# Two convolution tiles moved from retention into the merge, and layer 1's retention low parts moved to VectorE

## The chip, the cores and the metric

The kernel runs on one core of a Trainium2 chip. The metric is the device time of one execution in microseconds (us). Before the change three runs took 2858.27, 2862.72 and 2868.04 us; the median is 2862.72. The engines that matter here are TensorE (PE in the rows: matmuls), VectorE (DVE), ScalarE (ACT) and GpSimd (POOL). Each works through its own list of instructions in a fixed order.

## The reference

The reference is a two-layer transformer for diffusion. The token stream has 256 latent and 256 context rows of 1024 channels. In each layer one projection of the modulated stream feeds three mixing branches: a retention with 8 heads in two directions, an attention, and a convolution. The branches are gated, projected and summed; then comes a mixture of 64 small experts. What the change touches are the first and the third branch:

```python
scores = jnp.einsum('bnihd,bnjhd->bnhij', qc, kc) * decay_in          # retention, per head
y_inner = jnp.einsum('bnhij,bnjhe->bnihe', scores, vc)
...
br_ret = (jax.nn.silu(g) * layernorm_per_head(y)) @ w_ret_o

def conformer_conv(u, w_dw, b_dw, ln_g, ln_b):
    a, gte = jnp.split(u, 2, axis=-1)
    glu = a * jax.nn.sigmoid(gte)
    y = depthwise_conv(glu, w_dw, width=31) + b_dw                    # 1024 channels
    return jax.nn.silu(layer_norm(y, ln_g, ln_b))                     # norm over all channels

out = (sigmoid(g_ret) * br_ret + sigmoid(g_att) * br_att + sigmoid(g_conv) * (conv @ w_conv_o)) @ w_out
```

Layer 0 computes all 512 rows, layer 1 in the branches only the 256 latent ones (context rows enter as keys and values).

## The kernel before

*Weights in two parts.* Every float32 weight comes from memory as a piece `raw` of 128 partitions. ScalarE copies its high part to `whi` (L90), and VectorE or GpSimd subtracts that to give the low part `wlo` (L91), 128x1024 at a time. A matmul in L228 is then three matmuls: high by high, high by low, low by high. Which engine makes the low parts is set by a count: inside `split_on_pool(n)` every n-th low part goes to GpSimd, with n = 1 all of them, with n = 0 none. `SHARE` holds n for retention ("ret") and attention ("att"), one number for each layer; the merges of retention and convolution run under `split_on_pool(3)`.

*Retention* (L607 on) goes through 8 heads in four pairs. For a pair it projects keys, queries, values and a gate; for each head VectorE makes two decay masks (`ml` L619, `m2` L620, added by GpSimd in L621 and L629, exponentials by ScalarE in L622), multiplies the scores by them (`sa`, L683), and scales and splits the head's output (`ry` L696 and L697, `bT` L91). TensorE's mean of squares of a head is L693. After each pair the function yields, and the caller places work of the convolution there.

*Convolution.* The 1024 channels are eight tiles of 128. `conv_tile(t)` projects a tile (48 matmuls), gates it (`G`, L565, two buffers) and has VectorE run 31 taps over it: L569 and then 30 times L572, summed in one PSUM buffer `cacc`, the last into `cy`. The taps carry a lower priority than the rest (`CONV_BACK`), so the scheduler fills VectorE's list with them where other work has none. When all eight are there, `conv_norm` sums the tiles on GpSimd (`csum`, L584 and L586), takes the mean on TensorE (L580), subtracts it (L589), squares (L591), adds (L593), takes the second mean (L580), and scales (L597) and activates (L598). `conv_out` splits the result into parts, and the merge of the convolution reads them.

*The merge.* `merge(0, ...)` projects retention's output in four steps, each with a gate and a part of the adaLN projection. The norm of the convolution is placed ahead of its last step (L471). Then `merge(2, ...)` does the same with the convolution's output.

*The order of the work.* The program's order gives priorities; a scheduler turns these into one fixed list per engine when the kernel is built. So moving a call moves instructions on every engine. In layer 1 the weights' buffers are those of the whole kernel, in layer 0 the merge adds some of its own.

Of the kernel before, what the change touches and what calls it, by code (L numbers as in the profile page):

```python
# [31 lines left out]

ADA = {(0, 0): 2, (0, 2): 2, (0, 1): 0, (1, 0): 1, (1, 1): 0, (1, 2): 0}

SHARE = {"ret": (1, 1), "att": (1, 2)}
LN_EXP = list(get_activation_tables("")).index("natural_log_exp_and_others")

CAPS = {0: [256] * 2 + [192] * 7 + [128] * 19 + [64] * 36, 1: [192] + [128] * 11 + [64] * 52}
# [31 lines left out]
def body(ctx, tc, A, out):  # L70
# [12 lines left out]
    def pool_of(name, side=None):  # L83
        return tc.tile_pool(name=name, bufs=1, reuse_waits="tile", side=side)
# [11 lines left out]
    @contextmanager  # L96
    def split_on_pool(every):

        share.append(share[0])
        share[0] = every  # L100
        yield
        share[0] = share.pop()

    @contextmanager
    def weight_pool(name, raw, parts, own=False):


        with tc.tile_pool(name=name, bufs=1, reuse_waits="tile") as p:
            WP.append(dict(pool=p, raw=raw, parts=parts, own=own))
            yield  # L110
            WP.pop()
# [31 lines left out]
    def slab(ap):  # L143
        return chunk(ap, 4)
# [61 lines left out]
    def open_aux(n):  # L206

        aux_scope.close()
        aux_scope.enter_context(aux_banks(n))
# [3 lines left out]
    def bank(tag="mm", bufs=1):  # L213
        if tag == "mm":
            mm_turn[mms[-1]] = i = mm_turn.get(mms[-1], -1) + 1
            tag = f"mm{mms[-1][i % len(mms[-1])]}"
        pool_, bufs = aux[-1] if tag == "aux" else (ps, bufs)
        return pool_.tile([128, 512], F32, name=tag, tag=tag, bufs=bufs)

    def mm(o, a, b, start, stop):  # L220

        ops = []
        for x, y in zip(a, b):
            ops += [(x[0], y[0]), (x[0], y[1])]
            if len(x) == 2:
                ops.append((x[1], y[0]))
        for i, (l_, r_) in enumerate(ops):
            pe.matmul(o, l_, r_, start=start and i == 0, stop=stop and i == len(ops) - 1)  # L228
# [80 lines left out]
    def some(n):  # L309

        if n and later:
            ada(*later[:n])
            del later[:n]
            if not later:
                last_modulation()
# [47 lines left out]
    def actt(name):  # L363
        return wk.tile([128, 512], F32, name=name, tag="act", bufs=3)
# [29 lines left out]
    def row(name):  # L394
        return wk.tile([128, D], F32, name=name, tag="row", bufs=4)
# [23 lines left out]
    def mix(l):  # L419
        hT = [(hb[:, k], hb[:, 8 + k]) for k in range(8)]  # L420
        NQ = 512 if l == 0 else T
        NT = NQ // 128
        NS = NQ // T

        def wi(s):
            return ready.pop((l, s), None) or slab(A["w_in"][l * 38 + s])

        def wo(i, s):
            return slab(A["w_o"][(l * 4 + i) * 4 + s])

        def projT(w, n):

            o = [bank(), bank()]
            for h in range(2):
                for c in range(2):
                    mm(o[c][:, :n], [tuple(z[:, k, c * 128:c * 128 + 128] for z in w[h]) for k in range(4)],
                       [tuple(z[:, :n] for z in hT[4 * h + k]) for k in range(4)], h == 0, h == 1)
            return o

        def proj(w, src, nt):  # L440

            o = [bank().rearrange("p (a b) -> p a b", a=2) for _ in range(nt // 2)]
            for t in range(nt):
                for h in range(2):
                    mm(o[t // 2][:, t % 2], [tuple(z[:, t * 128:t * 128 + 128] for z in src[4 * h + k]) for k in range(4)],
                       [tuple(z[:, k] for z in w[h]) for k in range(4)], h == 0, h == 1)
            return o

        merged, sigmoids = [], {}
        with pool_of(f"mix{l}") as M:  # L450
            def newT():
                return [tuple(M.tile([128, NQ], FR, name="bT", tag="bT", bufs=16) for _ in range(2)) for _ in range(8)]

            def gates(br, s):

                gate = projT(wi(S_GT + br * 4 + s), NQ)
                sg = []
                for i in range(2):
                    sg.append(actt("sg")[:, :NQ])
                    sigmoids[i] = act.activation(sg[i], gate[i][:, :NQ], AF.Sigmoid)  # L460
                return sg

            def keep_gate(s, gate):

                sg = actt("sg")[:, :NQ]
                act.activation(sg, gate[:, :NQ], AF.Copy)
                sp.dma_start(gd[s, :, :NQ], sg)

            def merge(br, bT, between=None):
                for s in range(4):  # L470
                    if between and s == 3:  # L471
                        between()
                    if br == 1:
                        sg = []
                        for i in range(2):
                            sg.append(actt("sg")[:, :NQ])
                            act.dma_start(sg[i], gd[2 * s + i, :, :NQ])
                            act.activation(sg[i], sg[i], AF.Sigmoid)
                    else:
                        sg = gates(br, s)  # L480
                        some(ADA[l, br])
                    w = wo(br, s)
                    b = [bank(), bank()]
                    for h in range(2):
                        for c in range(2):
                            mm(b[c][:, :NQ], [tuple(z[:, k, c * 128:c * 128 + 128] for z in w[h]) for k in range(4)],
                               [bT[4 * h + k] for k in range(4)], h == 0, h == 1)
                    for i in range(2):
                        if len(merged) < 8:
                            if i == 0:  # L490
                                mg = row("mg")
                            m = mg[:, i * NQ:i * NQ + NQ]
                            dve.tensor_tensor(m, b[i][:, :NQ], sg[i], op=OP.mult)
                            merged.append(m)
                        else:
                            m = merged[2 * s + i]
                            dve.tensor_tensor(sg[i], b[i][:, :NQ], sg[i], op=OP.mult)
                            (dve if br == 1 and s == 3 else pool).tensor_tensor(m, m, sg[i], op=OP.add)
                    some(ADA[l, br])

            open_aux(1)
            with pool_of(f"conv{l}") as PC:
                conv_tile, conv_norm, conv_out = conv(l, PC, NQ, NS, lambda t: projT(wi(S_CU + t), NQ), newT)
                with pool_of(f"ret{l}") as P, split_on_pool(SHARE["ret"][l]):
                    bT = newT()
                    for p in retention(l, P, NQ, NS, NT, lambda s, nt: proj(wi(s), hT, nt),
                                       lambda s: projT(wi(s), NQ), bT):
                        conv_tile(2 * p)
                        conv_tile(2 * p + 1)
                with weight_pool(f"w_merge{l}", *((2, 3), (0, 0))[l]), split_on_pool(3):  # L510
                    merge(0, bT, conv_norm)
                    merge(2, conv_out(newT()))
            open_aux(2)
            with pool_of(f"att{l}") as P, split_on_pool(SHARE["att"][l]):
                bT = newT()
                attention(l, P, NQ, NS, NT, bT, hT, keep_gate, sigmoids.values())
                merge(1, bT)

        return merged
# [1282 lines left out]
    for t in range(4):  # L1802
        for c in range(2):
            p = bank("tr", 2)
# [15 lines left out]
    for l in range(L):  # L1820
        with weight_pool(f"w_mix{l}", l, l):
            merged = mix(l)
        moe(l, merged, A["tokens"] if l == 0 else xd)
# [89 lines left out]
```

## Time and profile before

| | before |
|---|---|
| median of 3 runs | 2862.72 us (2858.27 to 2868.04) |
| profiled execution | 2861.13 us |
| its span, first to last instruction | 2859.3 us |
| mean granted clock of TensorE | 0.944 |
| TensorE busy | 2582.9 us, 90% |
| VectorE busy | 1660.0 us, 58% |
| ScalarE busy | 1307.7 us, 46% |
| GpSimd busy | 673.6 us, 24% |

The profiled execution has 1.8 us outside its span. "Busy" is the time in which an engine has an instruction running; an instruction that is held up while it runs counts as busy. The granted clock is the share of TensorE's full 2.4 GHz that the chip let it have; 0.5 is its lower level of 1.2 GHz. Retention of layer 0 lies at about 90 to 346 us, its first merge to 441; in layer 1 they lie at 1695 to 1905 and on to 1969.

### The profile page before, as it was taken

How to read it: one execution, taken by the hardware profiler on the slowest of the kernel's cores; microseconds unless marked ns; L12 is line 12 of the kernel's file. 1: busy time of each engine (PE TensorE's matmuls, PEld its weight loads, DVE VectorE, ACT ScalarE, POOL GpSimd, SP SyncE). 2: the span in 40 equal slices, each digit the busy share in tenths (PEclk: the TensorE clock that was granted, in tenths of full speed). 3: DMA queues.
4: the chain of work that ended last, by engine and by line, in shares of the span. 5: the costliest groups of instructions: out<-in, count | busy, mean ns of one | idle time of the engine just before them, and what ended most of it. 6: DMA issues, size and time to landing. Idle time of an engine off the chain costs nothing. (4 is left out here: it accounts for less than half of the span.)

```text
span 2859.3 us, 39759 instructions
## 1 busy us (share of the span) xinstructions
PE 2582.9 (90%) x14811; PEld 1872.1 (65%) x14811; DVE 1660.0 (58%) x2963; ACT 1307.7 (46%) x2388; POOL 673.6 (24%) x449
## 2 busy tenths in 40 slices
PE   6999999999997899999999478888989799999995
PEld 5887777788777655555555268877978655554552
DVE  4588895258847555555555487887587722231223
ACT  3444425247732355555555236445476333343331
POOL 2444311222234111212121045532312300000000
PEclk7999999999998899999999798889999899999997
DMA  5212256621162599999999742235415399999996
GB/s 217 74 60 74 97 204 229 235 77 52 63 207 82 219 373 401 405 391 393 397 379 391 297 168 89 89 118 193 163 65 183 121 389 420 419 366 397 416 415 255
DMA packets 130055, 685.18 MB, mean 240 GB/s; under 512 B 22080, under 2 KB 37056, under 8 KB 56896
## 3 DMA queue, kind: packets, MB, share of 16 engines
q1 hardware_dynamic: 103344, 624.80, 56.1%
q0 software_dynamic: 20496, 41.98, 3.9%
q10 hardware_dynamic: 6016, 15.80, 1.4%
q8 instruction: 119, 1.95, 0.3%
q14 instruction: 80, 0.66, 0.1%
HBM read 651.76 MB, written 62.98 MB: 250 GB/s over the span
## 5 line engine op out<-in xcount | busy, mean ns | idle before, releaser
L90 ACT ACTIVATE whi<-raw 128x1024 fp32r<-128x1024 f32 x444 | 457.6, 1053 | 266.3 <-PE mm L228 149.9
L91 POOL TENSOR_TENSOR wlo<-raw,whi 128x1024 fp32r<-128x1024 f32 x140 | 344.4, 2469 | 723.3 <-ACT whi L90 653.8
L91 DVE TENSOR_TENSOR wlo<-raw,whi 128x1024 fp32r<-128x1024 f32 x304 | 375.0, 1254 | 204.1 <-ACT whi L90 200.7
L228 PE MATMUL mm<-whi,hb 128*128 128x256 f32 (+1 forms) x2080 | 428.9, 302 | 34.1 <-ACT whi L90 9.2
L228 PE MATMUL mm<-hb,whi 128*128 128x512 f32 (+1 forms) x1536 | 402.2, 349 | 14.8 <-ACT whi L90 6.0
L228 PEld LDWEIGHTS mm<-whi,hb 128*128 128x128 f32 x2080 | 349.7, 202 | 45.0 <-issue 14.2
L1544 PE MATMUL mm<-raw,xw 128*64 128x512 f32 x1408 | 332.8, 600 | 0.9 <-DMA raw<-in_w_exp 0.9
L1614 POOL DMA_INDIRECT y<-y,ix x94 | 95.7, 1018 | 977.8 <-ACT y L1610 867.1
L228 PE MATMUL mm<-wlo,hb 128*128 128x256 f32 (+1 forms) x1040 | 312.9, 301 | 11.4 <-POOL wlo L91 7.9
L228 PEld LDWEIGHTS mm<-hb,whi 128*128 128x128 f32 x1536 | 269.6, 195 | 51.8 <-ACT whi L90 6.6
L572 DVE SCALAR_TENSOR_TENSOR cacc<-G,cpk,cacc 128x512 f32<-128x512 f32 (+1 forms) x464 | 287.4, 619 | 10.3
L228 PE MATMUL mm<-hb,wlo 128*128 128x512 f32 (+1 forms) x768 | 268.7, 351 | 4.2 <-POOL wlo L91 3.5
L228 PE MATMUL mm<-whi,xp 128*128 128x512 f32 x736 | 264.4, 413 | 1.7 <-ACT whi L90 1.7
L228 PEld LDWEIGHTS mm<-wlo,hb 128*128 128x128 f32 x1040 | 209.6, 202 | 15.8 <-POOL wlo L91 8.8
L1544 PEld LDWEIGHTS mm<-raw,xw 128*64 128x64 f32 x1408 | 94.4, 136 | 165.1 <-issue 158.2
L228 PE MATMUL mm<-bT,whi 128*128 128x512 f32 (+1 forms) x768 | 193.5, 342 | 0.6 <-DVE bT L91 0.2
L1106 DVE SCALAR_TENSOR_TENSOR hidp<-mm,tab,sgl 128x256 f32<-128x256 f32 x86 | 41.6, 483 | 237.0 <-ACT sgl L1102 236.1
L228 PEld LDWEIGHTS mm<-whi,xp 128*128 128x128 f32 x736 | 140.8, 191 | 51.0 <-ACT whi L90 9.4
L91 DVE TENSOR_TENSOR xp<-tr,xp 128x512 fp32r<-128x512 f32 (+2 forms) x126 | 59.6, 492 | 192.7 <-ACT xp L90 161.3
L1610 ACT ACTIVATE y<-mm 128x512 f32<-128x512 f32 (+1 forms) x188 | 110.3, 594 | 130.6 <-PE mm L1601 69.5
L228 PE MATMUL mm<-wlo,xp 128*128 128x512 f32 x400 | 161.6, 404 | 7.1 <-DVE wlo L91 6.9
L228 PEld LDWEIGHTS mm<-hb,wlo 128*128 128x128 f32 x768 | 149.5, 195 | 24.7 <-POOL wlo L91 4.4
(654 smaller groups left out, 4357.0 us busy)
## 6 DMA issues: line engine op xcount, KB each, us to landing
raw<-in_w_exp SPq DMA_DIRECT2D x384, 1024.0 KB
raw<-in_w_in SPq DMA_DIRECT2D x76, 1024.0 KB
raw<-in_w_ada SPq DMA_DIRECT2D x48, 1024.0 KB
raw<-in_w_o SPq DMA_DIRECT2D x32, 1024.0 KB
yb<-y SPq DMA_DIRECT2D x24, 1024.0 KB
mod<-modrow SPq DMA_DIRECT2D x12, 512.0 KB
raw<-in_w_shared SPq DMA_DIRECT2D x6, 1024.0 KB
x1d<-xr ACTq DMA_DIRECT2D x6, 512.0 KB
```

Source lines behind the costliest of these rows:

```text
L90: act.activation(hi, src, AF.Copy)
L91: eng.tensor_tensor(lo, src, hi, op=OP.subtract)
L228: pe.matmul(o, l_, r_, start=start and i == 0, stop=stop and i == len(ops) - 1)
L572: dve.scalar_tensor_tensor(v(y if j == 30 else acc), G[:, :, j:j + T], cpk[:, t, j:j + 1], v(acc), op0=OP.mult, op1=OP.add)
L1106: dve.scalar_tensor_tensor(o[:n], b[:n, 256:512], gate[:n], sg[:n], op0=OP.mult, op1=OP.mult)
L1544: pe.matmul(os_[s][0][half], xhs[s][0](k)[:, half], raws[index[r, i // 2]][:, k % 4 * 512:k % 4 * 512 + 512], start=k == 0, stop=k == 7)
L1610: act.activation(ys[b][:n, c * 512:c * 512 + 512], o[c], AF.Copy)
L1614: pool.indirect_dma_start(out=y8s[s, b][:], in_=ys[b][:n], in_offset=None, out_offset=bass.IndirectOffsetOnAxis(ap=tabs[s][b][1][:n, 1:2], ...
```

## The change

One number in `SHARE` changes: in layer 1's retention no low part goes to GpSimd, all are made by VectorE. And the convolution's tiles are spread in another way, in both layers: before, two after each of the four pairs of heads; now two, one, two and one, and the last two tiles ahead of the first two steps of the retention's merge, where the low parts are shared by `split_on_pool(3)`. `conv_norm` stays ahead of the last step. From L515 on lines are 8 higher in the changed kernel (L580 becomes L588).

```diff
-SHARE = {"ret": (1, 1), "att": (1, 2)}
+SHARE = {"ret": (1, 0), "att": (1, 2)}
...
             def merge(br, bT, between=None):
                 for s in range(4):
-                    if between and s == 3:
-                        between()
+                    if between:
+                        between(s)
...
                     for p in retention(l, P, NQ, NS, NT, lambda s, nt: proj(wi(s), hT, nt),
                                        lambda s: projT(wi(s), NQ), bT):
-                        conv_tile(2 * p)
-                        conv_tile(2 * p + 1)
+                        for t in ((0, 1), (2,), (3, 4), (5,))[p]:
+                            conv_tile(t)
+
+                def rest(s):
+
+                    if s < 2:
+                        conv_tile(6 + s)
+                    if s == 3:
+                        conv_norm()
+
                 with weight_pool(f"w_merge{l}", *((2, 3), (0, 0))[l]), split_on_pool(3):
-                    merge(0, bT, conv_norm)
+                    merge(0, bT, rest)
                     merge(2, conv_out(newT()))
```

On VectorE, in the first pair of heads of layer 1's retention, this stands before the change (`vs`, `vc`, `vl` belong to the values, `ml`, `m2`, `sa`, `sal` to the masks and scores; the number behind a name tells its instance):

```order
L656 TENSOR_REDUCE vs_15840<-mm0_15735 128x4
L657 SCALAR_TENSOR_TENSOR vc_15841<-vs_15840,mm0_15735 128x512
L620 TENSOR_SCALAR m2_15913<-delta_15501,lgx_159 128x512
L91 TENSOR_TENSOR vl_15833<-vc_15841,vh_15832 128x512
L625 TENSOR_TENSOR ml_15911<-ml_15911,cst_78 128x128 x2
L683 SCALAR_TENSOR_TENSOR sa_15932<-tr_15925,ml_15503 128x512
L683 SCALAR_TENSOR_TENSOR sa_15951<-tr_15944,mx_15504 128x512
L619 TENSOR_SCALAR ml_15975<-delta_15501,lg_125 128x512
```

The same place with the change:

```order
L664 TENSOR_REDUCE vs_15840<-mm0_15735 128x4
L91 TENSOR_TENSOR wlo_16042<-raw_16039,whi_16041 128x1024
L665 SCALAR_TENSOR_TENSOR vc_15841<-vs_15840,mm0_15735 128x512
L628 TENSOR_SCALAR m2_15913<-delta_15501,lgx_159 128x512
L91 TENSOR_TENSOR wlo_16046<-raw_16039,whi_16045 128x1024
L91 TENSOR_TENSOR wlo_16141<-raw_16138,whi_16140 128x1024
L91 TENSOR_TENSOR vl_15833<-vc_15841,vh_15832 128x512
L691 SCALAR_TENSOR_TENSOR sa_15932<-tr_15925,ml_15503 128x512
L633 TENSOR_TENSOR ml_15911<-ml_15911,cst_78 128x128 x2
L691 SCALAR_TENSOR_TENSOR sa_15951<-tr_15944,mx_15504 128x512
L627 TENSOR_SCALAR ml_15975<-delta_15501,lg_125 128x512
```

Three low parts of weights, each behind a high part that ScalarE has to make first, now stand between the values and the first scores.

On VectorE, where layer 1's convolution ends (the last taps into `cy`, then the subtraction of the mean), before:

```order
L493 TENSOR_TENSOR mg_18459<-mm1_18409,sg_18373 128x256
L572 SCALAR_TENSOR_TENSOR cacc_17949<-G_17944,cpk_15480,cacc_17949 128x256 x2
L493 TENSOR_TENSOR mg_18459<-mm2_18410,sg_18375 128x256
L572 SCALAR_TENSOR_TENSOR cacc_17949<-G_17944,cpk_15480,cacc_17949 128x256
L276 TENSOR_TENSOR modT_117<-aux_18475,bT_ada_80 128x4
L572 SCALAR_TENSOR_TENSOR cacc_17949<-G_17944,cpk_15480,cacc_17949 128x256
L91 TENSOR_TENSOR wlo_18544<-raw_18541,whi_18543 128x1024
L572 SCALAR_TENSOR_TENSOR cacc_17949<-G_17944,cpk_15480,cacc_17949 128x256 x2
L572 SCALAR_TENSOR_TENSOR cy_17948<-G_17944,cpk_15480,cacc_17949 128x256
L589 TENSOR_TENSOR cy_16105<-cy_16105,aux_18488 128x256
```

And with the change:

```order
L580 SCALAR_TENSOR_TENSOR cacc_17854<-G_17849,cpk_15480,cacc_17854 128x256 x8
L580 SCALAR_TENSOR_TENSOR cy_17853<-G_17849,cpk_15480,cacc_17854 128x256
L91 TENSOR_TENSOR wlo_18625<-raw_18622,whi_18624 128x1024
L577 TENSOR_SCALAR cacc_18120<-G_18115,cpk_15480 128x256
L91 TENSOR_TENSOR wlo_18629<-raw_18622,whi_18628 128x1024
L580 SCALAR_TENSOR_TENSOR cacc_18120<-G_18115,cpk_15480,cacc_18120 128x256 x10
L91 TENSOR_TENSOR wlo_18750<-raw_18743,whi_18749 128x1024
L580 SCALAR_TENSOR_TENSOR cacc_18120<-G_18115,cpk_15480,cacc_18120 128x256 x19
L580 SCALAR_TENSOR_TENSOR cy_18119<-G_18115,cpk_15480,cacc_18120 128x256
L597 TENSOR_TENSOR cy_16105<-cy_16105,aux_18488 128x256
```

Before, the gated products `mg` of the merge's third step stand among the last tile's taps; now all 30 of the last tile stand behind them, and the low parts for the last gate and for the next branch stand among these taps.

On TensorE, at the mean over the squares (`crs`) of layer 1's convolution, before (`mm3`, `mm0` with `bT` are products of the merge's last step):

```order
L228 MATMUL mm3_18632<-bT_15499,whi_18628 128x256
L228 MATMUL mm3_18632<-bT_15500,whi_18628 128x256
L228 MATMUL mm3_18632<-bT_15499,wlo_18629 128x256
L580 MATMUL aux_18521<-crs_18480,mean_d_102 128x256
L228 MATMUL mm0_18633<-bT_15485,whi_18624 128x256
L228 MATMUL mm0_18633<-bT_15486,whi_18624 128x256
L228 MATMUL mm0_18633<-bT_15485,wlo_18625 128x256
```

And with the change (`mm2` with `hb` is a gate of the next branch):

```order
L228 MATMUL mm2_18753<-hb_15175,whi_18749 128x256 x2
L228 MATMUL mm2_18753<-hb_15175,wlo_18750 128x256
L588 MATMUL aux_18488<-csum_18479,mean_d_102 128x256
L588 MATMUL aux_18521<-crs_18480,mean_d_102 128x256
L228 MATMUL mm0_18633<-bT_15485,whi_18624 128x256
L228 MATMUL mm0_18633<-bT_15486,whi_18624 128x256
L228 MATMUL mm0_18633<-bT_15485,wlo_18625 128x256
```

Before, 45 rows of products stood between the mean over the channels (`csum`) and that over the squares; now these products, and the next gate, stand ahead of the first of the two means, and the second follows it directly.

## Rows read from the trace of the kernel before

**Rows 1.** Busy time of each engine in the whole span, with its share and instructions.
```profile
PE 2582.9 (90%) x14811; PEld 1872.1 (65%) x14811; DVE 1660.0 (58%) x2963; ACT 1307.7 (46%) x2388; POOL 673.6 (24%) x449
```
**Rows 2.** Windows: length, PE, PEld, DVE, ACT, POOL busy, granted clock, DMA share, GB/s.
```profile
90.00:346.00 256.00, 243.65 (x1315) 201.60 (x1315) 208.43 (x299) 113.03 (x148) 102.48 (x60) 0.95 0.20 70
...
1695.00:1905.00 210.00, 181.25 (x1282) 171.65 (x1282) 168.23 (x310) 114.89 (x160) 108.75 (x64) 0.88 0.26 90
1905.00:1969.00 64.00, 53.02 (x448) 47.27 (x448) 55.70 (x109) 18.70 (x29) 12.75 (x9) 0.89 0.52 188
1969.00:1996.00 27.00, 22.48 (x167) 19.75 (x168) 18.49 (x36) 25.31 (x42) 3.84 (x2) 0.94 0.45 164
```
**Rows 3.** VectorE groups, 1690 to 1905: busy, mean ns, idle before, releasers.
```profile
L91 DVE TENSOR_TENSOR bT<-ry,bT 128x256 fp32r<-128x256 f32 x7 | 9.7, 1386 | 0.4
...
L683 DVE SCALAR_TENSOR_TENSOR sa<-tr,ml 128x512 f32<-128x512 f32 x8 | 5.5, 683 | 6.7 <-POOL ml L621 6.7
```
**Rows 4.** GpSimd groups, 1690 to 1905.
```profile
L91 POOL TENSOR_TENSOR wlo<-raw,whi 128x1024 fp32r<-128x1024 f32 x35 | 86.2, 2479 | 83.2 <-ACT whi L90 66.1 <-issue 15.2 <-POOL mx L629 1.0
L621 POOL TENSOR_TENSOR ml<-ml,m 128x512 f32<-128x512 f32 x8 | 11.4, 1424 | 0.4 <-POOL wlo L91 0.4
```
**Rows 5.** Timeline, GpSimd and VectorE: start us, us, engine, line, operation, idle before.
```profile
1695.80 2.40 POOL L91 TENSOR_TENSOR wlo<-raw,whi 128x1024 fp32r<-128x1024 f32 x1 [0.81 <-DVE rtmp L412]
1698.62 1.35 POOL L621 TENSOR_TENSOR ml<-ml,m 128x512 f32<-128x512 f32 x1 [0.42 <-POOL wlo L91]
...
1695.86 2.63 DVE L620 TENSOR_SCALAR m<-delta,lgx 128x512 f32<-128x512 f32 x1
1698.41 0.41 DVE L413 TENSOR_TENSOR z<-z,rtmp 128x256 f32<-128x256 f32 x1
...
1719.16 0.49 DVE L620 TENSOR_SCALAR m<-delta,lgx 128x512 f32<-128x512 f32 x1
```
**Rows 6.** Waits of TensorE, 1695 to 1905: total us, times, longest.
```profile
PE tr L228 <- DVE sa L683: 8.2, 5, 4.6
```
**Rows 7.** Timeline of VectorE around layer 1's first merge.
```profile
1905.30 0.42 DVE L696 TENSOR_TENSOR ry<-mm,rs 128x256 f32<-128x256 f32 x1
...
1910.16 1.22 DVE L91 TENSOR_TENSOR wlo<-raw,whi 128x1024 fp32r<-128x1024 f32 x1
1911.30 5.21 DVE L572 SCALAR_TENSOR_TENSOR cacc<-G,cpk,cacc 128x256 f32<-128x256 f32 x10
...
1967.45 0.48 DVE L572 SCALAR_TENSOR_TENSOR cy<-G,cpk,cacc 128x256 f32<-128x256 f32 x1
1969.60 0.75 DVE L589 TENSOR_TENSOR cy<-cy,aux 128x256 f32<-128x256 f32 x2 [1.67 <-PE aux L580]
```
**Rows 8.** Timeline of TensorE at layer 1's two means and behind.
```profile
1968.86 0.70 PE L580 MATMUL aux<-csum,mean_d 128*128 128x256 f32 x2 [0.29 <-POOL csum L586]
...
1977.40 0.70 PE L580 MATMUL aux<-crs,mean_d 128*128 128x256 f32 x2
...
1995.71 0.39 PE L228 MATMUL mm<-bT,whi 128*128 128x256 f32 x2
```
**Rows 9.** Timeline of VectorE, layer 0: last head's scaling, last tap.
```profile
346.13 0.69 DVE L696 TENSOR_TENSOR ry<-mm,rs 128x512 f32<-128x512 f32 x1 [0.33 <-ACT rs L243]
...
435.20 0.74 DVE L572 SCALAR_TENSOR_TENSOR cy<-G,cpk,cacc 128x512 f32<-128x512 f32 x1
```
**Rows 10.** Timeline of TensorE, layer 0's merge: matmuls, and the mean.
```profile
392.46 0.63 PE L228 MATMUL mm<-hb,whi 128*128 128x512 f32 x2
...
393.16 0.63 PE L228 MATMUL mm<-hb,whi 128*128 128x512 f32 x2
...
440.39 1.02 PE L580 MATMUL aux<-csum,mean_d 128*128 128x512 f32 x2
```
**Rows 11.** Waits of VectorE, 1900 to 2070.
```profile
DVE wlo L91 <- ACT whi L90: 24.6, 15, 4.6
```
**Rows 12.** VectorE groups, 1905 to 1970.
```profile
L91 DVE TENSOR_TENSOR wlo<-raw,whi 128x1024 fp32r<-128x1024 f32 x8 | 12.9, 1621 | 0.7 <-ACT whi L90 0.7
```

## The prediction, made before the changed kernel ran

> **What bounds the kernel now.** I read the page's busy times first, then the mixing stages in a table by windows, then what stretches and what waits there, and last the timeline at the two places where the convolution ends.
>
> TensorE is busy 2582.9 us of the span, VectorE 1660.0 [rows 1]. The sum over the program therefore says TensorE, but the change touches four stretches only: retention of layer 0 (90 to 346 us) and of layer 1 (1695 to 1905), and the first merge behind each. The reader should see in [rows 2] how different the two layers are. Retention of layer 0 leaves TensorE 256.0 - 243.65 = 12.35 us idle. Retention of layer 1 leaves 210.0 - 181.25 = 28.75 us idle and runs at a granted clock of 0.88: both its own 256 columns and its waits are short, and VectorE's 168.2 us are nearly as long as TensorE's work. In the first merge of layer 1 VectorE is busy 55.7 of 64 us and is the one that is waited for: TensorE's mean over the channel sums stands at 1968.86 [rows 8], right behind the last tap, and all that follows of the convolution hangs on it.
>
> In retention of layer 1 some of VectorE's busy time is not work. GpSimd makes 35 low parts there in 86.2 us [rows 4]. While it made the one at 1695.80, VectorE's scaling of `delta` took 2.63 us; the same instruction took 0.49 at 1719.16 [rows 5]. The group `bT<-ry,bT` has a mean of 1.386 us, while the convolution's taps, of the same width and with their sum in PSUM, keep to ten in 5.21 [rows 7]. Summed over the order of VectorE's instructions at quiet prices (tap 0.52, low part 1.14, both from one start to the next [rows 7], the others at their quiet rows), retention up to the last head is 148.6 us of work; the busy time is 168.2 and the stretch 210: 19.6 us are stretched instructions and 41.8 us idle. Of the idle time 6.7 us end with GpSimd's sum of the decay mask, `sa<-POOL ml` [rows 3]; that sum stood behind a low part in GpSimd's queue at 1695.80 and 1698.62 [rows 5]. TensorE in turn waits 8.2 us for `sa` [rows 6].
>
> The Trainium skill, "SBUF — State Buffer", section "SBUF: two separate sides", says that a GpSimd instruction and a VectorE instruction with two inputs in SBUF (or in a two-port mode) take one port pair as a lock, and the later one blocks for the whole of the other. Stretched subtractions beside unstretched taps agree with it. By that rule the 16 sums that GpSimd keeps could still block as much as they last.
>
> **The change, part by part.** First, low parts of layer 1's retention. In the new order 34 of them stand between VectorE's retention instructions; at 1.14 us that is 39 us more work on VectorE and 84 us less on GpSimd. GpSimd keeps two sums per head: eight took 11.4 us [rows 4], so I put all 16 at 22. What of the 19.6 us of stretch stays lies between 0 and those 22; I take 3, because the sum at 1698.62 stands beside an instruction of 0.41 us [rows 5].
>
> Second, the tiles. A tile is 48 matmuls and 31 taps. With 512 columns three matmuls start in 393.16 - 392.46 = 0.70 us [rows 10], so one is 0.233 us, and I take half, 0.117 us, for the 256 columns of layer 1. Counted in the two orders, 50 matmuls leave the stretch up to the last head of layer 0 (11.7 us), and 33 that of layer 1 (3.9 us). Fewer than two tiles' 96, since part of the last tile stood behind the last head already and other work moves up. VectorE's work behind the last head grows from 84.6 us (to the last tap) to 111.4 in layer 0, and from 54.9 to 84.0 in layer 1; before the last head of layer 1 it is 160.1 instead of 148.6: 39 us of low parts come and 27 us of taps and GLUs go.
>
> *Layer 0.* The last head's scaling is at 346.13, the last tap ends at 435.94 [rows 9]: 84.6 us of work took 89.8. With 111.4 I take 117.4. The head comes earlier by 11.7 us and by what TensorE no longer waits, 0 to 12.35; with 26 us less on VectorE before it I take 8 of these, in all 20. So the last tap ends at 346.1 - 20 + 117.4 = 443.5, and the mean follows after 0.9 as in layer 1 [rows 7, 8], at 444.4; before it was at 440.39 [rows 10], with the sum of channels lying ready. That is +4.0. Nine more matmuls stand in front of it, so 2.1 us less behind: +1.9. Bounds: +10 with nothing of the waits back, -2 with all.
>
> *Layer 1.* From the last head's scaling at 1905.30 to the first subtraction of the mean at 1969.60 [rows 7] are 64.3 us for 54.9 of work, 9.4 over. With 84.0 it is 93.4: +29.1. Against that stands how much earlier the last head comes. VectorE: 160.1 of work, 3 of stretch, and of 41.8 idle I leave 32 (6.7 go with GpSimd's queue, 3 come by the new waits below, and low parts fill some holes): 195 instead of 210, so 15 us. TensorE agrees with that size: 3.9 us of matmuls and 11 of its 28.75 idle. Bounds: 0, when new waits eat all, and 32, when 17 of the idle and half of what the clock takes (0.12 x 181 = 22 us) come back.
>
> Behind the mean the order on TensorE is new. Before, 45 rows stood between the mean over the channels and the mean over the squares, and they filled the 8.5 us between 1968.86 and 1977.40 [rows 8]. Now nothing stands between them: what did has moved ahead, so TensorE stands idle through both the wait for the last taps and this chain. In front of the mean are 80 more matmuls (9.4 us); of the 22.5 us of work between 1969 and 1996 [rows 2] 13.1 stay. From the mean to the first matmul of the convolution's output, 1995.71 - 1968.86 = 26.9 us, it becomes 8.5 + 13.1 = 21.6, where I take -4.5 as some waits stay, and +1 for TensorE's clock, which the windows show under its full level of 2.4 GHz where it waits (granted 0.88 in retention, 0.89 in the merge [rows 2]). Layer 1: 29.1 - 15 - 4.5 + 1 = +10.6.
>
> *New waits.* A low part on VectorE waits for ScalarE's high part, and with it all that is queued behind: taps, scores' `sa`, the head's scaling. Where VectorE is busy this cost 0.7 us for 8 pieces [rows 12], 0.09 each; where it is not, 24.6 us for 15 [rows 11], 1.64 each. For 34 that is 3 to 56 us. I take 3, the row in which VectorE is as full as it will be here.
>
> The Trainium skill, "Perfetto Trace Analysis", section "Optimizing Scalar/DVE Operations", advises to take work off a VectorE that is saturated, and adds that giving it to GpSimd may not help since both share a port. The change goes against the first half; the stretched rows speak for the second.
>
> **Sum.** The profiled execution took 2861.1 us, 1.6 under the median of the runs shown. 2861.1 + 1.9 + 10.6 = 2873.6; I forecast 2873.
>
> **Rivals.** *Relief* (other side). GpSimd's low parts cost more than their stretch: they hold back the decay sums, hence `sa`, hence TensorE and its clock. Place: retention of layer 1; price 17 us of idle, 11 of clock and the 3.9 moved, 32; layer 0 gets its waits back too. 29.1 - 32 - 4.5 = -7.4 and -2.1: 2851.6, say 2852. It decides from about 26 us on, where layer 1 comes out even. For it: waits for `sa` and the stretch are the largest items [rows 3, 6]. Against: VectorE would have to do 160 us of work in 178, with less idle than it has anywhere now.
>
> *Low parts at the head of VectorE's queue.* Each waits for its high part 0.35 us or more, between the two rows above; 12 us of that use up all that the stretch gave, and the last head stays at 1905. 29.1 - 4.5 + 1 + 1.9 = +27.5: 2889. For it: 24.6 us of such waits [rows 11]. Against: 0.7 us where VectorE was full [rows 12].
>
> *Nothing.* TensorE's work is the same, and what is moved fills holes elsewhere: 2861. Against it: VectorE's work up to the mean grows by 245.0 - 204.4 = 40.6 us in a stretch in which it is already waited for.
>
> **How the numbers follow.** Under 0.3% (8.6 us) a measurement of this kernel can't be told from no change, so faster is below 2854, slower above 2870. Forecast 0.45, own range 2862 to 2886: most of it slower (0.28), some the same (0.15), 0.02 faster. Relief 0.28: 0.25 faster, 0.03 the same. Head of queue 0.17: slower. Nothing 0.10: 0.08 the same, 0.02 faster. Together faster 0.29, same 0.26, slower 0.45. The range reaches from a little below relief to the head of queue, 2848 to 2891.
>
> **What would show it.** The window from layer 1's first decay to its last head 15 us shorter, VectorE's groups there back at quiet means (`bT<-ry,bT` near the 0.42 of the scaling beside it [rows 7]) and 34 low parts of 1.2 us; the time from the last head to the mean near 93 us instead of 64; TensorE idle some 8 us between its two means and about as long ahead of the first; in layer 0 the mean near 444. Wrong: waits of `wlo` for `whi` of more than 10 us in retention (head of queue), or a last head more than 26 us earlier (relief).

## The result: 0.63% slower, and the profile after

The changed kernel took 2880.82 us (median of 5 runs, 2879.68 to 2883.06) against 2864.81 for the kernel before beside it: a ratio of 1.0063, 95% interval 1.0048 to 1.0079, or 16 us. The forecast was 2873, slower, with 2848 to 2891 as the range. The profiled execution took 2882.63 us, 21.5 more than that of before. Where do these 21.5 us arise? I compare starts of the same instruction in the two timelines:

| | before | after | later by |
|---|---|---|---|
| layer 0, last head's scaling `ry` | 346.13 | 331.77 | -14.4 |
| layer 0, mean subtracted | 441.45 | 453.91 | +12.5 |
| layer 0, first sum of the experts' outputs, `yb` | 1606.41 | 1620.80 | +14.4 |
| layer 1, first decay | 1695.46 | 1707.72 | +12.3 |
| layer 1, last head's scaling | 1905.30 | 1888.28 | -17.0 |
| layer 1, mean subtracted | 1969.60 | 1986.87 | +17.3 |
| layer 1, last `aqT` of attention | 2147.17 | 2171.66 | +24.5 |
| layer 1, last sum of the experts' outputs, `yb` | 2842.61 | 2864.07 | +21.5 |

So in this pair of executions layer 0 loses about 14 us, and layer 1, from its first decay on, another 12 up to the last `aqT` and 9 up to the end. The last stretch, from there to the end, is the same code in every run here and takes 692 to 699 us, so these last 3 us are chance. In both layers the last head comes much earlier, and more than that is lost behind it.

The windows of the profile after, with bounds moved to the same events [rows 2] (length; PE, PEld, DVE, ACT, POOL busy; granted clock, DMA share, GB/s):

```profile
90.00:332.00 242.00, 233.07 (x1269) 194.31 (x1268) 187.33 (x271) 109.46 (x145) 92.68 (x54) 0.94 0.21 74
332.00:454.00 122.00, 111.55 (x619) 83.89 (x619) 109.36 (x149) 27.39 (x37) 21.79 (x14) 0.96 0.48 179
1708.00:1888.00 180.00, 166.01 (x1222) 156.85 (x1221) 155.94 (x293) 109.16 (x155) 31.11 (x25) 0.93 0.29 100
1888.00:1986.00 98.00, 75.02 (x584) 66.68 (x583) 81.57 (x161) 25.32 (x37) 20.68 (x17) 0.87 0.48 172
1986.00:2015.00 29.00, 14.29 (x87) 11.56 (x87) 12.28 (x34) 24.18 (x40) 0.52 (x1) 0.68 0.11 37
```

The reader is to see two things. Layer 1's retention (third row) became short and full: 180 us instead of 210, TensorE idle 14 instead of 28.75, granted clock 0.93 instead of 0.88. The two rows below pay for it: TensorE is idle 23 of 98 us and 15 of the next 29, where before it was idle 11 of 64 and 4.5 of the next 27.

VectorE's groups in layer 1's retention, with the low parts on it, from 1702 to 1888 (busy, mean ns, idle before, releasers):

```profile
L91 DVE TENSOR_TENSOR wlo<-raw,whi 128x1024 fp32r<-128x1024 f32 x33 | 43.7, 1326 | 7.0 <-ACT whi L90 7.0
...
L691 DVE SCALAR_TENSOR_TENSOR sa<-tr,ml 128x512 f32<-128x512 f32 x8 | 5.5, 683 | 2.6 <-POOL ml L629 2.6
...
L91 DVE TENSOR_TENSOR bT<-ry,bT 128x256 fp32r<-128x256 f32 x7 | 3.0, 432 | 0.5 <-ACT bT L90 0.3
```

`bT<-ry,bT` fell from 1386 to 432 ns and the wait for the mask from 6.7 to 2.6 us [rows 3]: most of the stretch is gone. The 33 low parts waited 7.0 us for their high parts.

Layer 0, TensorE at the first weights of the merge, and at the mean [rows 10]:

```profile
335.38 0.97 PE L228 MATMUL mm<-hb,whi 128*128 128x512 f32 x3 [2.25 <-ACT whi L90]
343.75 0.80 PE L228 MATMUL mm<-hb,wlo 128*128 128x512 f32 x1 [7.41 <-DVE wlo L91]
...
452.75 1.12 PE L588 MATMUL aux<-csum,mean_d 128*128 128x512 f32 x2 [0.29 <-POOL csum L594]
```

And VectorE over the same first stretch:

```profile
331.77 0.69 DVE L704 TENSOR_TENSOR ry<-mm,rs 128x512 f32<-128x512 f32 x1 [1.32 <-ACT rs L243]
...
336.28 6.29 DVE L580 SCALAR_TENSOR_TENSOR cacc<-G,cpk,cacc 128x512 f32<-128x512 f32 x8
342.48 1.22 DVE L91 TENSOR_TENSOR wlo<-raw,whi 128x1024 fp32r<-128x1024 f32 x1
...
453.91 1.29 DVE L597 TENSOR_TENSOR cy<-cy,aux 128x512 f32<-128x512 f32 x2 [2.64 <-PE aux L588]
```

At the mean itself TensorE waits only 0.29 us. It lost its time earlier: a low part of a moved tile's weights, made by VectorE now, stands in the list behind eight taps, and TensorE stood 7.41 us for it. Before, TensorE had no idle time at all from 346 to 441:

```profile
346.00:441.00 95.00, 95.00 (x561) 72.10 (x559) 83.85 (x116) 23.38 (x33) 17.90 (x10) 1.00 0.59 216
```

Layer 1, TensorE at the two means and at the first matmul of the convolution's output [rows 8]:

```profile
1985.61 1.22 PE L588 MATMUL aux<-csum,mean_d 128*128 128x256 f32 x2 [7.25 <-POOL csum L594]
1992.63 1.22 PE L588 MATMUL aux<-crs,mean_d 128*128 128x256 f32 x2 [5.80 <-DVE crs L601]
...
2013.20 1.01 PE L228 MATMUL mm<-bT,whi 128*128 128x256 f32 x3 [8.00 <-ACT whi L90]
```

Here TensorE does wait for the last taps (7.25), then for the squares (5.80), and then 8.00 for a high part of a weight that ScalarE made only behind the activations of the convolution:

```profile
2008.66 0.59 ACT L606 ACTIVATE cy<-cy,cpk 128x256 f32<-128x256 f32 x1
...
2010.22 1.28 ACT L460 ACT_TABLE_LOAD   x1
2011.52 0.39 ACT L460 ACTIVATE sg<-mm 128x256 f32<-128x256 f32 x1
2011.80 0.41 ACT L90 ACTIVATE bT<-cy 128x256 fp32r<-128x256 f32 x1
2012.10 1.05 ACT L90 ACTIVATE whi<-raw 128x1024 fp32r<-128x1024 f32 x1
```

### The profile page after: what moved, and what is told of

Its sections match the earlier page's. It is cut to its first block, busy times and chain, and to the rows that moved or that the text cites. A ratio compares the mean times of both kernels' runs of the same rounds, so it can differ in the third digit from the quotient of the medians.

```text
span 2880.8 us, 39746 instructions
## 1 busy us (share of the span) xinstructions
PE 2585.0 (90%) x14811; PEld 1870.6 (65%) x14811; DVE 1676.7 (58%) x3003; ACT 1308.7 (45%) x2387; POOL 579.7 (20%) x409
## 5 line engine op out<-in xcount | busy, mean ns | idle before, releaser
L91 DVE TENSOR_TENSOR wlo<-raw,whi 128x1024 fp32r<-128x1024 f32 x344 | 427.2, 1260 | 227.3 <-ACT whi L90 223.8
L228 PE MATMUL mm<-hb,whi 128*128 128x512 f32 (+1 forms) x1536 | 408.1, 353 | 19.4 <-ACT whi L90 13.5
L91 POOL TENSOR_TENSOR wlo<-raw,whi 128x1024 fp32r<-128x1024 f32 x100 | 247.5, 2482 | 602.1 <-ACT whi L90 561.8
L580 DVE SCALAR_TENSOR_TENSOR cacc<-G,cpk,cacc 128x512 f32<-128x512 f32 (+1 forms) x464 | 287.5, 620 | 9.5
L228 PE MATMUL mm<-hb,wlo 128*128 128x512 f32 (+1 forms) x768 | 268.7, 351 | 10.3 <-DVE wlo L91 8.3
```

What stands on the lines that cost most here:

```text
L91: eng.tensor_tensor(lo, src, hi, op=OP.subtract)
L580: dve.scalar_tensor_tensor(v(y if j == 30 else acc), G[:, :, j:j + T], cpk[:, t, j:j + 1], v(acc), op0=OP.mult, op1=OP.add)
```

## The experiments

Theory A, after the traces: the loss comes from moving the tiles, and the low parts on VectorE pay for themselves. Theory B, its rival: 39 us more work on VectorE is the loss. Four runs take the change apart.

**SHARE alone.** `SHARE["ret"]` is (1, 0), tiles as before.

> Only the number in SHARE changes; the tiles stay two after each pair of heads in both layers. Theory A (the loss comes from moving the tiles; VectorE's work up to the mean of layer 1 is what its retention and merge last, and the freed stretch pays for the 39 us of low parts): layer 0 keeps its times, layer 1 comes out 0 to 8 us earlier than before, total 2853 to 2865. Theory B (the loss comes from 39 us more work on a VectorE that is already waited for): layer 1 some 10 us later, total 2870 to 2880.

**Tiles alone, both layers.** `SHARE["ret"]` stays (1, 1).

> Only the tiles move, in both layers; GpSimd keeps all low parts of layer 1's retention. Theory A: layer 0 loses what it lost with the whole change (12 to 14 us at the mean over the channels), and layer 1, whose VectorE stretch stays and whose last head comes only some 8 us earlier, loses 10 to 20 more: 2885 to 2900. Theory B: layer 1 loses nothing without the low parts on VectorE: about 2875.

**Tiles in layer 0 alone.** `SHARE["ret"]` stays (1, 1).

```diff
-                        for t in ((0, 1), (2,), (3, 4), (5,))[p]:
+                        for t in (((0, 1), (2,), (3, 4), (5,)) if l == 0 else ((0, 1), (2, 3), (4, 5), (6, 7)))[p]:
...
-                    if s < 2:
+                    if l == 0 and s < 2:
```

> The tiles move in layer 0 alone; all else as before. Theory A: the loss of layer 0 stands by itself, +12 to +15 us, 2874 to 2880, with the same two waits of TensorE for the first weights of the merge (about 2 us for the high part and 7 for the low part) as in the changed kernel. Rival: the shift of layer 0 is given back later, in attention or the experts, whose weights come by DMA at its full rate: within 5 us of before.

**SHARE, and tiles in layer 1 alone** (the same edit with `l == 1`, on top of the change).

> SHARE as in the change, and the tiles move in layer 1 alone; layer 0 as before. Theory A: what the change took in layer 1 stands by itself, +5 to +9 us, 2866 to 2874. Against the run with SHARE alone it says what the moved tiles do to layer 1: theory A says they lose there, 8 to 14 us; the rival says that the early last head (29 us earlier) makes them gain or do nothing, so this run is no slower than the one with SHARE alone.

The three stretches, from the timelines ("retention" from layer 1's first decay to its last head's scaling, "tail" from the last head's scaling to the first subtraction of the mean; us), and the ratios:

| run | layer 0 tail | layer 1 retention | layer 1 tail | both | median, us | ratio to before, 95% |
|---|---|---|---|---|---|---|
| before | 95.3 | 209.8 | 64.3 | 274.1 | 2864.81 | 1 |
| changed | 122.1 | 180.6 | 98.6 | 279.1 | 2880.82 | 1.0063 [1.0048, 1.0079] |
| SHARE alone | 95.3 | 200.7 | 77.3 | 278.0 | 2860.92 | 0.9989 [0.9972, 1.0006] |
| tiles alone | 122.2 | 194.4 | 88.1 | 282.5 | 2887.68 | 1.0077 [1.0053, 1.0100] |
| tiles in layer 0 | 122.9 | 208.1 | 64.1 | 272.2 | 2874.23 | 1.0030 [1.0016, 1.0045] |
| SHARE, tiles in layer 1 | 95.3 | 178.9 | 98.7 | 277.7 | 2867.32 | 1.0010 [0.9993, 1.0027] |

(The medians of before beside these four runs, 2863.58, and beside the next ones are within 2.7 us of that in the first row.)

B falls by the times: SHARE alone costs nothing that can be told from zero, and tiles alone cost at least as much as both together (the two intervals overlap). All four medians lie in the ranges that A gave, the layer-0 run at the edge of its own (2874.23; its profiled execution, at 2865.78, was among the shortest), and that run has the two waits that A named, 2.2 and 7.4 us. Not all of A is shown. In the trace of SHARE alone layer 1 is not 0 to 8 us earlier: from its first decay to its last `aqT` it takes 458.6 us, against 451.7 before and 449.8 in the run with tiles in layer 0, whose layer 1 is that of before. This trace is of an execution 6.4 us above its median, so that the low parts pay for themselves rests on the medians alone. How the 18 us of the ratio divide is open too: by the medians the tiles of layer 0 take 8.6 us (4.6 to 12.9), and SHARE with tiles in layer 1 takes 2.9, not clear of zero; by the traces the latter makes layer 1 some 12 us longer (463.9 in the changed kernel, 462.3 in that run).

The tails are the steadiest numbers of the study: layer 0's is 95.3 or 122 to 123, by whether the tiles move there, in every run. In layer 1 each edit alone shortens retention (9 and 15 us, both 29) and lengthens the tail (13 and 24 us, both 34); what is saved ahead of the last head comes back behind it. The last expectation missed in part: that the moved tiles lose 8 to 14 us against SHARE alone. They lose 6.4 by the medians, which the two intervals do not part from zero, and nothing up to the mean (277.7 against 278.0).

**What makes the tail.** Theory V: VectorE's work behind the last head. Theory W: TensorE's waits for the first weights of the merge, whose low parts came to VectorE's list with the moved tiles. The first run takes these low parts off VectorE, the second takes taps off it, the third does both.

```diff
                     if s < 2:
-                        conv_tile(6 + s)
+                        with split_on_pool(1):
+                            conv_tile(6 + s)
```

> The changed kernel, but the low parts of the two moved tiles' weights are all made by GpSimd (in the change two of three are VectorE's). Theory W (TensorE loses time at the first weights of the merge, 2.2 us for a high part and 7.4 for a low part that stands behind eight taps on VectorE): these waits go in layer 0, the mean over the channels comes 6 to 10 us earlier there, total 2868 to 2874. Theory V (VectorE's work behind the last head sets the mean): only the five or six low parts fall away, 1.14 us each, 6 us in layer 0 and in layer 1, and TensorE waits for the sum of channels at the mean instead: 2870 to 2876.

```diff
-                for j in range(1, 31):
-                    dve.scalar_tensor_tensor(v(y if j == 30 else acc), G[:, :, j:j + T], cpk[:, t, j:j + 1], v(acc),
+                n = 16 if t > 5 else 31
+                for j in range(1, n):
+                    dve.scalar_tensor_tensor(v(y if j == n - 1 else acc), G[:, :, j:j + T], cpk[:, t, j:j + 1], v(acc),
```

> The changed kernel, with the last 15 taps of channel tiles 6 and 7 left out (both layers), so 30 taps less on VectorE behind the last head: 23.6 us in layer 0, 15.5 in layer 1; TensorE's work is the same. Theory V: layer 0 loses nothing any more (mean at about 440) and layer 1 gains 8 to 15 at its mean: 2845 to 2860. Theory W: TensorE still waits for its weights ahead of the mean; layer 0 keeps 8 to 12 us of its loss, 2862 to 2874.

> Both edits at once: low parts of the moved tiles by GpSimd, and the last 15 taps of tiles 6 and 7 left out. Theory V: nothing beyond the run with fewer taps. Theory W: nothing beyond the run with GpSimd's low parts but a few us. If both bind at the same time, only here does layer 0 come back in full, and this run is faster than either by 5 us or more.

And a dose: one tile moved instead of two, `((0, 1), (2, 3), (4, 5), (6,))[p]` and `conv_tile(7)` ahead of the first step.

> The changed kernel with one tile moved instead of two: two tiles after each of the first three pairs, one after the last, tile 7 ahead of the merge's first step. Theory V: the loss goes with the work behind the last head; of the 27 us more in layer 0 about half come, and the last head comes 5 to 8 us earlier, so layer 0 loses 5 to 8 and the total is 2864 to 2872. The rival (any new weights in the merge cost TensorE a wait): the same waits as with two tiles, 2874 or more.

| run | layer 0 tail | layer 1 retention | layer 1 tail | median, us | ratio to before, 95% |
|---|---|---|---|---|---|
| changed | 122.1 | 180.6 | 98.6 | 2880.82 | 1.0063 [1.0048, 1.0079] |
| low parts by GpSimd | 118.7 | 178.7 | 94.4 | 2868.80 | 1.0032 [1.0018, 1.0047] |
| 30 taps left out | 119.6 | 180.3 | 80.6 | 2857.00 | 0.9982 [0.9970, 0.9994] |
| both | 118.5 | 181.7 | 73.2 | 2845.63 | 0.9950 [0.9933, 0.9967] |
| one tile moved | 106.4 | 199.9 | 78.9 | 2873.18 | 1.0040 [1.0027, 1.0052] |

Layer 0 answers clearly. With 23.6 us of taps gone from VectorE its tail shrinks by 2.5 us, and TensorE's two waits are the same within 0.01 us. In the run without the 30 taps:

```profile
331.46 0.97 PE L228 MATMUL mm<-hb,whi 128*128 128x512 f32 x3 [2.24 <-ACT whi L90]
339.84 0.80 PE L228 MATMUL mm<-hb,wlo 128*128 128x512 f32 x1 [7.41 <-DVE wlo L91]
```

With the low parts on GpSimd, TensorE waits less there:

```profile
331.93 1.22 PE L228 MATMUL mm<-hb,whi 128*128 128x512 f32 x2 [2.24 <-ACT whi L90]
334.46 0.80 PE L228 MATMUL mm<-hb,wlo 128*128 128x512 f32 x1 [1.31 <-POOL wlo L91]
```

The layer's tail is TensorE's own. Its busy and idle time there, beside VectorE's busy time (us):

| run | layer 0 tail | TensorE busy | TensorE idle | VectorE busy |
|---|---|---|---|---|
| before | 95.3 | 95.3 | 0 | 83.9 |
| changed | 122.1 | 111.7 | 10.5 | 109.5 |
| low parts by GpSimd | 118.7 | 111.8 | 6.9 | 106.7 |
| 30 taps left out | 119.6 | 109.3 | 10.3 | 88.3 |
| both | 118.5 | 111.8 | 6.7 | 85.7 |

V falls there: with both edits VectorE has 23.8 us less to do, and the tail is only 3.6 us shorter. Of the 26.8 us that the change added, 59 matmuls more behind the head, at 0.233 us, are 13.7, and TensorE's idle time is 10.5, 9.7 of it the two waits. I put the other 2.6, time in which TensorE was busy, to the clock, which was at half in the changed kernel from 336.6 to 346.9, without a run that shows it. W has the place right, and its size only in part. With the low parts on GpSimd the mean comes 6.9 us earlier, in W's range, but 3.5 of these are there at the last head already. Of the two waits 6.1 us go, and 2.8 come back as a wait of TensorE for VectorE's `modT` (3.3 us instead of 0.5), so the tail gets back 3.5.

Layer 1 is the other way round. Taking 15.5 us of taps away shortens its tail by 18.0. The two ends of that tail on VectorE, in the run without the 30 taps:

```profile
1877.33 0.42 DVE L705 TENSOR_TENSOR ry<-mm,rs 128x256 f32<-128x256 f32 x1
...
1957.91 1.41 DVE L598 TENSOR_TENSOR cy<-cy,aux 128x256 f32<-128x256 f32 x4 [1.66 <-PE aux L589]
```

TensorE waits 0.4 us for the sum of channels at the mean there, and 7.25 in the changed kernel. Low parts on GpSimd give 4.2, both edits 25.4. V holds in layer 1, and since layer 1 gave more than V's 8 to 15, the total (2857.00) lies in V's range although layer 0 kept its loss. As to the totals, the two edits add up (by the ratios 9 and 23 us alone, 32 together). So the run with both is faster than either by more than 5 us, as "both bind at once" had it, but layer 0 does not come back in it, and that theory is not needed; V's and W's "nothing beyond" fell as well. The run with both is no better kernel, since half the taps of two tiles are missing.

One tile moved brings half a way in layer 0's tail, 106.4 (TensorE busy 100.6), with waits of 2.15 and 1.82 us, so the rival's "same waits" missed. Its mean is subtracted at 453.69, 12.2 us later than before, since the last head did not come earlier (347.33); but the trace is of the longest of the run's 12 executions (2880.58), and the time of a head carries some us of chance (last section). The total, 2873.18, lies between V's range and the rival's. So this run does not decide whether the loss goes by the number of tiles.

**A better version?** The runs point to layer 1's merge: VectorE is waited for there, and its taps, with their sum in PSUM, don't stretch beside GpSimd. So I gave that merge's low parts to GpSimd, tiles as before, with all, none and half of the retention's on VectorE:

```diff
-                    merge(0, bT, conv_norm)
+                    with split_on_pool(1 if l else 3):
+                        merge(0, bT, conv_norm)
```

> The kernel before, with SHARE as in the change (layer 1's retention low parts by VectorE), the tiles as before, and in layer 1's retention merge all low parts by GpSimd instead of one in three. If VectorE's work behind the last head sets layer 1's mean (theory V), and its taps, with their sum in PSUM, are not stretched by GpSimd, some eight low parts of 1.14 us leave the tail: the mean 6 to 10 us earlier than with SHARE alone, total 2850 to 2857. Rival: GpSimd's low parts are late for TensorE (2.5 us each, three buffers) and its sums of channels queue behind them: 2862 to 2870.

> The kernel before, with only layer 1's retention merge on GpSimd for all low parts; SHARE and tiles as before. Theory V: the tail from the last head to the first subtraction of the mean, 64 us for 55 us of work, loses 9 us of low parts, but TensorE then arrives second: 4 to 8 us earlier, 2855 to 2860. Rival: as in the run beside it, 2866 to 2872.

> As the first of these three, but in layer 1's retention every second low part goes to GpSimd. Half of the low parts cost VectorE 20 us instead of 39 and leave half of the stretch. If the two costs are each linear, it lies between its neighbours, 2852 to 2860. If the decay sums queued behind low parts are what matters (theory R, relief), it is nearer to the run without low parts on GpSimd in what retention lasts.

| run | layer 1 retention | layer 1 tail | both | mean to last `aqT` | median, us | ratio to before, 95% |
|---|---|---|---|---|---|---|
| before | 209.8 | 64.3 | 274.1 | 177.6 | 2864.81 | 1 |
| SHARE alone | 200.7 | 77.3 | 278.0 | 180.6 | 2860.92 | 0.9989 [0.9972, 1.0006] |
| all on VectorE in retention | 198.9 | 73.8 | 272.7 | 183.3 | 2865.00 | 1.0009 [0.9994, 1.0025] |
| none | 206.7 | 59.2 | 266.0 | 184.7 | 2866.43 | 1.0018 [1.0005, 1.0032] |
| half | 207.4 | 63.9 | 271.2 | 181.3 | 2863.04 | 1.0008 [0.9994, 1.0022] |

None beats the kernel before, and all three expectations missed; the first two times lie in the rival's ranges. The tails did shrink, by 3.5 us (against SHARE alone) and 5.1 (against before), and the taps kept their 488 ns beside 12 low parts on GpSimd:

```profile
L573 DVE SCALAR_TENSOR_TENSOR cacc<-G,cpk,cacc 128x256 f32<-128x256 f32 x97 | 47.4, 488 | 3.0
...
L91 POOL TENSOR_TENSOR wlo<-raw,whi 128x1024 fp32r<-128x1024 f32 x12 | 28.3, 2384 | 29.3 <-ACT whi L90 20.2 <-PE aux L273 9.1
```

but nothing of it reached the end. A part went as the rival had it. TensorE's waits for GpSimd's low parts, 1890 to 2000, with SHARE alone:

```profile
PE mm L228 <- POOL wlo L91: 2.9, 2, 1.7
```

and with the merge's low parts on GpSimd too (total us, times, longest):

```profile
PE mm L228 <- POOL wlo L91: 7.1, 5, 1.9
```

By the traces the rest went behind the mean. From the first subtraction of the mean to the last `aqT` of attention the run with none of the low parts on VectorE takes 7.2 us more than before, of the 8.1 it had gained up to there; the run with all of them takes 2.7 more than SHARE alone, of 5.3; the run with half takes 3.7 more than before, where it had gained 2.9. Work had moved there: in the run with all, 46 matmuls fewer than with SHARE alone stand in the tail, and 49 more behind it. In the run with none, TensorE is busy 16.0 of the first 26.3 us behind the mean, and was 21.8 before. Single runs of before beside these lie between 2854 and 2872, and a gain of some us is at the edge of what their medians show. With half of the low parts on GpSimd retention is nearly as long as with all there (207.4; 206.7 and 209.8 with all, 198.9 and 200.7 with none), so most of the loss comes with the first half.

## Why the prediction was right, and where it was wrong

The direction, the time within its range, and layer 1 as the place where saved time comes back were right. Two steps failed: in layer 0 what sets the mean, and in layer 1 the chain behind the mean. In layer 1 an error of opposite sign hid it, and the sum looks better than its working.

- **Layer 0 (+1.9, measured +14.4 at the layer's end).** Of the 12.5 us between, 5.6 are the head, 2.7 the way from it to the mean, and 4.0 what was to be saved behind it and was not. The head came 14.4 us earlier, not 20: the matmuls moved away gave their 11.7, but of the idle time 3.4 us came back, not 8 (242.00 - 233.07 = 8.93 idle against 12.35). This term carries chance: the head is at 341.1 to 348.6 us in the six traces with the old order, and at 323.0 to 331.8 in the six with two tiles moved, 16.7 earlier in the mean. The failed step is the mechanism: I let VectorE's work set the mean and TensorE arrive early. The 117.4 us for that were near the 122.1 measured only because TensorE, with 13.7 us more matmuls and 9.7 of new waits, takes about as long. That these two nearly agree is luck. I had priced waits of VectorE's low parts for their high parts, but not TensorE's wait for a low part behind taps, and I had put new waits in layer 0 at nothing, without a reason. Nor had I added up TensorE's own list behind the head, although before the change it had no idle time there. The runs without 30 taps show that VectorE's taps are not what binds there.
- **Layer 1, ahead of the last head (-15, measured -29.3).** The bounds were 0 and 32, and the relief case was the nearer one. Stretch: 3 us stayed, as taken: 33 low parts of 1.326 instead of 1.22 us are 3.5 us. (The row I took them from shows little: the instruction of 0.41 us had begun 0.21 before GpSimd's sum.) New waits for high parts took 7.0 us, not 3. But VectorE's other idle time fell much more than the 10 us that I allowed: 24.1 us in the window (180.00 - 155.94) against 41.8. And VectorE was busy 155.9 us there, where work and stretch were put at 163. What held the clock at 0.88 before is open; it is 0.93 where TensorE idles 14 us instead of 28.75.
- **Layer 1, behind it (+29.1, measured +34.3)**, with waits of 6.7 us for adaLN's `aux` that were 1.7 before. The run without 30 taps shows that VectorE's work is what sets most of this tail.
- **The chain behind the mean (-4.5 and +1 for the clock).** TensorE's idle places came as forecast, 7.25 us ahead of the first mean and 5.80 between the two (forecast: about 8 each). But the shorter chain did not come: from the first subtraction to the first matmul of the convolution's output are 26.3 us, and were 26.1, since TensorE ran out of work and waited 8.00 us for a high part. So this step failed. The loss goes with the order: up to the last `aqT` the stretch takes 177.6 us in both traces with the old order and SHARE in layer 1, and 182.7 to 185.8 in the six with two tiles moved there, each with a wait of 8.0 to 8.4 us for the high part. And the clock cost more than 1 us. In the next three stretches of the same work, before and after:

```profile
1996.00:2035.00 39.00, 38.63 (x322) 38.23 (x322) 17.51 (x23) 20.47 (x27) 18.79 (x15) 1.00 0.62 210
2035.00:2100.00 65.00, 56.98 (x427) 54.02 (x426) 47.12 (x94) 36.01 (x70) 9.41 (x8) 0.95 0.27 96
2100.00:2155.00 55.00, 48.37 (x360) 44.20 (x360) 52.12 (x109) 43.54 (x98) 12.18 (x6) 1.00 0.26 87
```

```profile
2013.00:2054.00 41.00, 39.23 (x302) 38.62 (x303) 21.61 (x23) 19.37 (x28) 19.09 (x15) 0.92 0.50 174
2054.00:2122.00 68.00, 59.98 (x436) 57.12 (x435) 46.30 (x92) 36.55 (x68) 9.07 (x7) 0.90 0.28 98
2122.00:2179.00 57.00, 50.52 (x369) 46.75 (x369) 53.38 (x110) 44.97 (x100) 12.52 (x6) 0.97 0.24 84
```

  The granted clock is 0.92, 0.90 and 0.97 where it was 1.00, 0.95 and 1.00, and 166 us pass instead of 159. That the idle places ahead of it lowered the clock is what the order in time suggests; no run took it apart.
- **The rivals.** Relief happened as far as its place goes: its sign, a last head more than 26 us earlier, was met within the layer (29.3), and still layer 1 came out slower, since the tail and the chain behind the mean took more than the sum had. "Low parts at the head of the queue" did not happen (7.0 us of waits, and the head came earlier). Of layer 1 my sum said +10.6, and from its first decay to its last `aqT` it lost 12.2. That is near by chance: up to the mean the sum said +14.1 and it was +5.0 (-29.3 + 34.3), and behind the mean it said -3.5 and it was +7.2. (VectorE's 245.0 and 204.4 us of work up to the mean, under "Nothing", are 0.9 more than the sums of their parts, 244.1 and 203.5; their difference is right.)

## What to carry to other kernels

When work moves from one side of a fixed point (here the last head) to the other, time both sides: an early head is worth nothing if the list behind it grew by as much. Look up, for each side, which engine sets its length: in layer 0 it was TensorE, with its own matmuls and its waits for weights that came through the other engine's list, in layer 1 VectorE's own work, and the same edit needed two different sums. A moved call takes its loads and its weights' preparation along, to an engine chosen by where it now stands; these come first in the new place, and wait there behind whatever is already queued.

## What the runs showed of the hardware

- The clock of TensorE differs from one execution to the next in a stretch whose instructions and order are the same. In layer 0's retention, window 155 to 185, before and in a run whose edits are in layer 1 only:

```profile
155.00:185.00 30.00, 29.32 (x121) 22.90 (x120) 22.46 (x36) 13.98 (x20) 10.07 (x7) 0.77 0.13 42
```

```profile
155.00:185.00 30.00, 29.32 (x147) 22.61 (x146) 27.26 (x44) 17.57 (x26) 9.74 (x7) 1.00 0.21 71
```

  TensorE is busy 29.32 us in both, with 121 matmuls at a granted clock of 0.77 and 147 at 1.00; the second run is 6.3 us ahead from there on. So the time of one head in one profile carries some 6 us of chance, while the tails of runs with the same order there were equal within 1 us.
- VectorE and GpSimd stretch each other, and not all instructions alike. Subtractions with both inputs in SBUF stretched (1386 ns against 432); taps, with one input in PSUM, kept 486 to 488 ns beside GpSimd's low parts. The Trainium skill, "SBUF — State Buffer", section "SBUF: two separate sides", counts instructions with two inputs in SBUF, and those in a two-port mode, among those that take the lock, and the rows of subtractions and taps agree. The scaling of `delta`, with one tensor input, stretched too (2.63 us against 0.49 [rows 5]); whether it ran in a two-port mode no row shows. And with VectorE making the low parts, GpSimd's sums of masks rose from 1.424 us [rows 4] to 1.644:

```profile
L629 POOL TENSOR_TENSOR ml<-ml,m 128x512 f32<-128x512 f32 x8 | 13.2, 1644 | 104.7 <-DVE m L628 97.0 <-ACT mx L635 7.7
```
